# Tiled transformer-style block on one core: high and low tokens of a half go through one stationary tile as one matmul of two 256-column runs, in the output projection and the first FFN pairs

## The chip, the core and the metric

The kernel runs on one core of one Trainium2 chip. The engines that matter here are TensorE (PE in the rows; its weight loads are PEld), VectorE (DVE), ScalarE (ACT), GpSimd (POOL, which here issues transfers) and the queue of SyncE (SPq), which issues most transfers. The metric is the device time of one execution in microseconds, lower is better.

## What is computed

One layer over 512 latent tokens and 256 context tokens, 2048 channels wide, in fp32: modulation vectors from a conditioning vector, a token mixer (two parallel scans), an output projection, and a SwiGLU feed-forward network. What the change touches, cut from the reference:

```python
y = jnp.concatenate([y_m, y_r], axis=-1).astype(u.dtype) @ w_out          # output projection
x = x + m_lat[2] * rms_norm(yx, g_post_mix[layer])
hx = rms_norm(x, g_pre_ffn[layer]) * (1.0 + m_lat[4]) + m_lat[3]
gu = u @ w_ffn_in                                                          # u is hx
(jax.nn.silu(gu[..., :D_FF]) * gu[..., D_FF:]) @ w_ffn_out
```

`m_lat[2]` to `m_lat[5]` are products of the conditioning vector with four 2048-column blocks of `w_mod`.

## The kernel before

**Split products.** Every fp32 operand of a large product is kept as a high part and a low part in the type float32r, and a product is made of high times high, high times low and low times high. `aHL` holds the activations, [128, 2, 16, 512]: high (`aH`) and low (`aL`), 16 channel tiles, 512 tokens. A weight tile of 128 x 1024 comes into one of three buffers `wr` by a transfer on SyncE's queue; ScalarE casts it to `wH` (line 170), VectorE subtracts to get `wL` (line 186). There are four pairs `wH`/`wL`; the fourth is called `w3H`/`w3L`.

**Units.** One weight tile is one unit: eight stationary 128 x 128 blocks. In the stage of this change, tokens are worked in two halves of 256 (`halves`). The output projection has 32 units for each half (16 output tiles `o`, two units each, `j`), then the first FFN pairs have 24 units for each half (6 pairs `f`, gate and up, two units each): 112 units in all. `chunk` issues a unit of a half as 24 matmuls of 256 columns: for each of eight blocks the high weights with high tokens, then the same high weights with low tokens, and after these the low weights with high tokens. The results of tile `o` go to `wbank(o)`, which alternates between two PSUM banks (`bank_66` for even `o`, `bank_65` for odd `o`), so tile `o + 2` overwrites the bank of tile `o`. Later stages use `wide`, which issues a unit as 8 matmuls of 512 columns (high and low tokens of 256) and 8 of 256.

**Order.** Nothing is scheduled on the chip: the program is written out engine by engine while the kernel is built, and each engine runs its instructions in that order. What order results is decided by a small planner with a clock for each engine (`clk`). `spend` adds a fixed cost for each instruction. The main stream is the units; everything else is written as generators in lanes: `E` the evacuations of PSUM, `N` the norms and the modulation (`chain`, `sums`), `W` the modulation vectors (`mod_lane`). After about every 510 planner ns of matmul, `slot` asks each lane whether its next step is placed here:

```python
for n, lim in cur[0].rate:
    while lanes[n] and due(lanes[n][0]) and max(clk["dve"], clk["act"]) - clk["pe"] < lim:
        step(n)
```

In the output projection the limit of `W` is `RWO = 1053` and of `N` `RNO = 2600`. A step that is needed at once is forced with `until`, which places the whole lane up to a flag there. While unit `i` is written out, casts are placed up to unit `i + 3` and low parts up to unit `i + 2`.

**The `W` lane.** `mod_lane` streams `w_mod` through a single buffer `wm` of 512 KB. Each of its 128 half steps is one VectorE instruction (line 457), which multiplies `wm` in place and sums it, and then a transfer on SyncE's queue that fills `wm` again (line 462). The instruction waits for the transfer before it, and the transfer for the instruction before it. A step of the lane is two halves.

**The `N` lane in this stage.** `chain(0)` runs beside the projection of the second half: it normalizes the first half of the projection, adds the residual, writes it out to DRAM (`xdr`, line 1042), takes the sum of squares, makes the second norm, then calls

```python
yield from norm(pb, [nsum[:, 0:HALF], nsum[:, HALF:S]])
until("W", ("mod", 2))
```

and makes the new high and low tokens in eight steps, one for two channel tiles: one VectorE multiply, two activations and one cast on ScalarE, one VectorE subtract. The first FFN unit of a half is preceded by `until("N", ("u", hf))`. `chain(1)` runs beside the pairs of the first half in the same way.

Of the kernel before, what the change touches and what calls it, by code (L numbers as in the profile page):

```python
# [8 lines left out]
AF = mybir.ActivationFunctionType  # L9
ALU = mybir.AluOpType  # L10
# [4 lines left out]
S = 512  # L15
# [5 lines left out]
HALF = S // 2  # L21
# [55 lines left out]
def build(tc, A):  # L77
# [6 lines left out]
    with pool as sb, ppool as ps, dpool as dr, tc.manual_schedule():  # L84
        bank = [ps.tile([128, 512], F32, name=f"bank{i}") for i in range(8)]
        aHL = sb.tile([128, 2, KT, S], F32R, name="aHL")
        cHL = sb.tile([128, 2, 8, S], F32R, name="cHL")
        aH, aL = aHL[:, 0], aHL[:, 1]
# [25 lines left out]
        modv = sb.tile([128, 4, KT], F32, name="modv")  # L114
# [14 lines left out]
        yx = lambda o: ya[0][:, S * o:S * o + S] if o < 8 else sz[:, S * (o - 8):S * (o - 8) + S]  # L129
# [28 lines left out]
        def width(ap):  # L158
            n = 1
            for d in ap.shape[1:]:  # L160
                n *= d
            return n

        def act(out, in_, f, **kw):
            spend("act", 220 + 0.833 * width(in_) + (2560 if f in (AF.Sqrt, AF.Ln) else 0))
            SC.activation(out, in_, f, **kw)  # L166

        def acopy(out, in_):
            spend("act", 220 + 0.833 * width(in_))
            SC.copy(out, in_)  # L170
# [13 lines left out]
        def tt(out, a, b, op):  # L184
            spend("dve", 70 + 1.04 * width(out))
            V.tensor_tensor(out, a, b, op)  # L186
# [9 lines left out]
        def mm(out, l, r, st, sp):  # L196
            spend("pe", 0.424 * width(r) * (1 if r.dtype == F32R else 4))
            PE.matmul(out, lhsT=l, rhs=r, start=st, stop=sp)  # L198
# [143 lines left out]
        for q in range(4):  # L342
            t = (sa if q < 2 else sz)[:, 2048 * (q % 2):2048 * (q % 2) + 2048]
# [549 lines left out]
        def chunk(H, L, jobs, slot):  # L893
            Hv, Lv = (t.rearrange("p (k f) -> p k f", f=128) for t in (H, L))
            for part in range(2):
                for out, mov, ks, first, last in jobs:
                    n = len(ks)
                    for kk, k in enumerate(ks):
                        h, l = mov(k)
                        if part == 0:  # L900
                            mm(out, Hv[:, kk], h, first and kk == 0, False)
                            mm(out, Hv[:, kk], l, False, False)
                        else:
                            mm(out, Lv[:, kk], h, False, last and kk == n - 1)
                        if clk["pe"] >= mark[0] + GAP:
                            mark[0] = clk["pe"]
                            slot()

        def wide(H, L, out, mov, slot):
            Hv, Lv = (t.rearrange("p (k f) -> p k f", f=128) for t in (H, L))  # L910
            out2 = out.rearrange("p (t s) -> p t s", t=2)
            for part in range(2):
                for k in range(8):
                    if part == 0:
                        mm(out2, Hv[:, k], mov(k), k == 0, False)
                    else:
                        mm(out2[:, 0], Lv[:, k], mov(k)[:, 0], False, k == 7)
                    if clk["pe"] >= mark[0] + GAP:
                        mark[0] = clk["pe"]
                        slot()  # L920

        lat = lambda k: (uH(k), uL(k))
        latp = lambda hs: (lambda k: (aH[:, k, hs], aL[:, k, hs]))
        ctxm = lambda k: (cHv[:, k, :], cLv[:, k, :])

        def pre_last0():
# [40 lines left out]
        nacc, nsqe = eb[2:4], eb[12]  # L967
# [100 lines left out]
        wbank = lambda o: bank[(len(order) + o) % 2]  # L1068
        for hf, hs in enumerate(halves):
            for o in range(KT):  # L1070
                for j in range(2):
                    def emit(H, L, slot, o=o, hs=hs, j=j):
                        ks = range(8 * j, 8 * j + 8)
                        chunk(H, L, [(wbank(o)[:, 0:HALF], latp(hs), ks, j == 0, j == 1)], slot)

                    def pre(o=o, hf=hf, j=j):
                        if o == 0 and hf == 0 and j == 0:
                            until("W", ("mod", 0))
                            flush_e()
                            ysplit_y(range(8, 16), halves[0])  # L1080
                            lane("N", ysplit_rest())
                        if hf == 0 and j == 0 and o == 10:
                            until("N", ("y", 15))
                        if hf == 1 and j == 0 and o == 0:
                            until("N", ("y", 11))

                    def post(o=o, hf=hf, hs=hs, j=j):
                        if j == 0:
                            return

                        def g():
                            if o == 0 and hf == 0:
                                until("N", ("y", 13))
                            y, b = yx(o)[:, hs], wbank(o)[:, 0:HALF]
                            act(nacc[hf] if o == 0 else nsqe, b, AF.Square)
                            act(y, b, AF.Copy, scale=modv[:, 0, o:o + 1])
                            yield
                            if o:
                                tt(nacc[hf], nacc[hf], nsqe, ALU.add)
                            if o == KT - 1:  # L1100
                                lane("N", chain(hf, bank[7 - hf]))
                                if hf:
                                    lane("N", sums())
                        lane("E", g())
                    add(A["wout"][o, 1 - j], 1024, emit, pre, post, (("W", RWO), ("N", RNO)))


        def first_pair(f, hf, pb, pre0):
            hs = halves[hf]
            g = gtmp[:, HALF * (f % 2):HALF * (f % 2) + HALF]  # L1110
            h = stmp[:, HALF * (f % 2):HALF * (f % 2) + HALF]

            def swiglu():
                bg, bu = pb[0][:, 0:HALF], pb[1][:, 0:HALF]
                act(g, bg, AF.Silu)
                yield
                tt(h, g, bu, ALU.mult)
                PL.dma_start(out=hdr[:, f, hs], in_=h)

            for gu in range(2):  # L1120
                for j in range(2):
                    def emit(H, L, slot, gu=gu, j=j):
                        chunk(H, L, [(pb[gu][:, 0:HALF], latp(hs), range(8 * j, 8 * j + 8), j == 0, j == 1)], slot)

                    def post():
                        lane("E", swiglu())
                        if hf and f == FIRST - 1:
                            flags.add("halves")

                    add(A["ffin"][f, gu, j], 1024, emit, pre0 if not (gu or j) else None, post if gu and j else None, (("N", RNF),))  # L1130
# [261 lines left out]
        for g, fs in enumerate(groups):  # L1392
            last = g == len(groups) - 1
# [213 lines left out]
```

## Time and profile before

| | us |
|---|---|
| median of 3 runs (lowest to highest) | 2518.44 (2515.88 to 2526.44) |
| the profiled execution, its own time | 2522.63 |
| its span, first to last instruction | 2520.9 |
| PE busy in the span | 2458.5 |
| the stage of the change, 921.5 to 1260.44 | 338.94 |
| in that stage PE / DVE / ACT busy | 332.06 / 243.76 / 194.72 |

Between the profiled time and its span lie 1.7 us outside the first and last instruction. The stage is read from the first 256-column matmul on `aHL` of the output projection to the first 512-column matmul of the next stage. A matmul's recorded duration is longer than the distance to the next one, since matmuls are pipelined; the distance between starts is what a stream of them costs.

### The profile page before, as it was taken

What the parts mean: (1) busy time and instruction counts of PE and PEld (TensorE: products, weight loads), DVE (VectorE), ACT (ScalarE), POOL (GpSimd) and SP (SyncE); (2) the same over time, 40 slices, a digit from 0 to 9 for tenths busy, and PEclk for the clock granted to TensorE, in tenths of its full rate; (3) what the DMA queues carried; (4) which work ended last, traced back from release to release, by engine and by line L of the source; (5) the groups of instructions that cost most, each with busy time, mean ns of one, the idle gap of its engine ahead of it and who ended that gap; (6) DMA issues with size and microseconds to landing.
All of it is one profiled execution on the core that took longest, in us unless ns stands there. A gap on an engine that the chain in (4) does not pass through costs nothing. (4 is left out here: it accounts for less than half of the span.)

```text
span 2520.9 us, 36962 instructions
## 1 busy us (share of the span) xinstructions
PE 2458.5 (98%) x14504; PEld 2149.3 (85%) x14504; DVE 1776.1 (70%) x2830; ACT 1064.2 (42%) x1466; POOL 194.7 (8%) x300
## 2 busy tenths in 40 slices
PE   6999999999999999999999999999999999999997
PEld 4688888888888889999988888888888888888897
DVE  4477576676767866768688888888888866633357
ACT  4353344444445445566444343333443351221254
POOL 0010000000000020101011111111111120000000
PEclk9999999999999999999999999999999999999998
DMA  8954434434343477867676666666666586643345
GB/s 326 371 200 134 146 102 145 136 103 138 122 138 108 152 237 248 284 186 235 205 203 165 173 169 167 181 176 164 171 169 182 155 297 224 214 134 92 100 152 192
DMA packets 129743, 453.56 MB, mean 180 GB/s; under 512 B 15936, under 2 KB 20032, under 8 KB 128672
## 3 DMA queue, kind: packets, MB, share of 16 engines
q1 hardware_dynamic: 102128, 358.02, 43.2%
q0 software_dynamic: 27440, 93.17, 14.3%
q8 instruction: 114, 1.87, 0.3%
q14 instruction: 61, 0.50, 0.1%
HBM read 383.49 MB, written 27.79 MB: 163 GB/s over the span
## 5 line engine op out<-in xcount | busy, mean ns | idle before, releaser
L198 PE MATMUL bank<-aHL,wH 128*128 128x512 f32 (+1 forms) x4792 | 1007.0, 356 | 8.1 <-ACT sa L166 2.5
L198 PEld LDWEIGHTS bank<-aHL,wH 128*128 128x128 f32 x4792 | 782.2, 191 | 124.8 <-issue 6.1
L170 ACT CAST wH<-wr 128x1024 fp32r<-128x1024 f32 (+2 forms) x335 | 345.1, 1031 | 511.0 <-PE bank L198 305.7
L198 PE MATMUL bank<-aHL,wL 128*128 128x256 f32 (+1 forms) x2856 | 543.3, 326 | 0.6 <-DVE wL L186 0.6
L198 PEld LDWEIGHTS bank<-aHL,wL 128*128 128x128 f32 x2856 | 436.9, 191 | 49.8 <-DVE wL L186 1.0
L186 DVE TENSOR_TENSOR wL<-wr,wH 128x1024 fp32r<-128x1024 f32 (+2 forms) x335 | 400.3, 1197 | 41.6 <-ACT wH L170 38.9
L186 DVE TENSOR_TENSOR sz<-sz,bank 128x256 f32<-128x256 f32 (+1 forms) x678 | 301.3, 450 | 125.6 <-PE bank L198 100.6
L198 PE MATMUL bank<-cHL,wH 128*128 128x256 f32 (+1 forms) x1536 | 294.1, 338 | 7.5 <-DVE cHL L186 3.5
L198 PEld LDWEIGHTS bank<-cHL,wH 128*128 128x128 f32 x1536 | 240.1, 190 | 40.5 <-ACT wH L170 4.1
L170 ACT CAST wH<-sz 128x1024 fp32r<-128x1024 f32 (+1 forms) x126 | 129.7, 1047 | 245.8 <-DMA sz<-sz 170.0
L457 DVE CUSTOM_DVE_ANT_0 wm<-wm,sil 128x1024 f32<-128x1024 f32 x128 | 156.1, 1220 | 72.2 <-DMA wm<-wm 72.2
L186 DVE TENSOR_TENSOR sz<-sz 128x512 f32<-128x512 f32 (+2 forms) x220 | 155.7, 710 | 70.9 <-DMA sz<-sz 40.3
L198 PE MATMUL bank<-aHL,w3H 128*128 128x256 f32 (+1 forms) x1064 | 194.6, 333 | 0.0
L198 PEld LDWEIGHTS bank<-aHL,w3H 128*128 128x128 f32 x1064 | 161.1, 191 | 16.9
L198 PE MATMUL bank<-cHL,wL 128*128 128x256 f32 (+1 forms) x992 | 163.2, 302 | 0.0
L198 PEld LDWEIGHTS bank<-cHL,wL 128*128 128x128 f32 x992 | 144.1, 190 | 18.9 <-DVE wL L186 5.3
L186 DVE TENSOR_TENSOR wL<-sz,wH 128x1024 fp32r<-128x1024 f32 (+1 forms) x126 | 152.7, 1217 | 7.8 <-ACT wH L170 6.3
L170 ACT CAST w3H<-wr 128x1024 fp32r<-128x1024 f32 (+1 forms) x75 | 77.0, 1027 | 174.5 <-PE bank L198 83.4
L198 PE MATMUL bank<-aHL,w3L 128*128 128x256 f32 (+1 forms) x680 | 105.4, 298 | 0.0
L198 PEld LDWEIGHTS bank<-aHL,w3L 128*128 128x128 f32 x680 | 95.6, 191 | 6.6
L166 ACT ACT_TABLE_LOAD x61 | 78.3, 1283 | 35.5 <-PE bank L198 29.8
L186 DVE TENSOR_TENSOR w3L<-wr,w3H 128x1024 fp32r<-128x1024 f32 (+1 forms) x75 | 89.2, 1190 | 2.0 <-ACT w3H L170 2.0
(230 smaller groups left out, 2168.5 us busy)
## 6 DMA issues: line engine op xcount, KB each, us to landing
wm<-wm SPq DMA_DIRECT2D x134, 512.0 KB, 3.7
wr<-ffin SPq DMA_DIRECT2D x105, 512.0 KB, 4.5
wr<-ffout SPq DMA_DIRECT2D x96, 512.0 KB, 3.6
sz<-ffin SPq DMA_DIRECT2D x95, 512.0 KB, 4.8
wr<-win SPq DMA_DIRECT2D x85, 512.0 KB, 3.6
wr<-wout SPq DMA_DIRECT2D x64, 512.0 KB, 4.5
sz<-sz POOLq DMA_DIRECT2D x38, 512.0 KB, 5.2
wr<-wm SPq DMA_DIRECT2D x20, 512.0 KB, 8.9
```

Of the source, the lines that this page charges most:

```text
L166: SC.activation(out, in_, f, **kw)
L170: SC.copy(out, in_)
L186: V.tensor_tensor(out, a, b, op)
L198: PE.matmul(out, lhsT=l, rhs=r, start=st, stop=sp)
L457: V.tensor_tensor_reduce(out=wm, in0=wm, in1=sil[:, 1024 * j:1024 * j + 1024], scale=1.0, scalar=0.0, op0=ALU.mult, op1=ALU.add, accum_out ...
```

## The change

In the 112 units of the output projection and of the first FFN pairs, `chunk` is replaced by `wide`: high and low tokens of the half are one matmul of 512 columns (two runs of 256), so a unit has 8 matmuls of 512 columns and 8 of 256 in place of 24 of 256. `wide` gets two flags, so that a sum may go over two units. High-weight products with high tokens and with low tokens now lie in two halves of a PSUM bank and have to be added: the evacuation of a projection tile becomes a copy by ScalarE, an add by VectorE that reads the other half of the bank, and then the square and the scaled copy, both from SBUF; before, square and scaled copy read PSUM and VectorE had no part in it but the running sum. The evacuation of a pair gets two copies and two adds. Bytes moved and columns streamed stay as they are.

```diff
-        def wide(H, L, out, mov, slot):
+        def wide(H, L, out, mov, slot, first=True, last=True):
             Hv, Lv = (t.rearrange("p (k f) -> p k f", f=128) for t in (H, L))
             out2 = out.rearrange("p (t s) -> p t s", t=2)
             for part in range(2):
                 for k in range(8):
                     if part == 0:
-                        mm(out2, Hv[:, k], mov(k), k == 0, False)
+                        mm(out2, Hv[:, k], mov(k), first and k == 0, False)
                     else:
-                        mm(out2[:, 0], Lv[:, k], mov(k)[:, 0], False, k == 7)
+                        mm(out2[:, 0], Lv[:, k], mov(k)[:, 0], False, last and k == 7)
...
                     def emit(H, L, slot, o=o, hs=hs, j=j):
-                        ks = range(8 * j, 8 * j + 8)
-                        chunk(H, L, [(wbank(o)[:, 0:HALF], latp(hs), ks, j == 0, j == 1)], slot)
+                        wide(H, L, wbank(o), lambda k: aHL[:, :, 8 * j + k, hs], slot, j == 0, j == 1)
...
                             if o == 0 and hf == 0:
                                 until("N", ("y", 13))
-                            y, b = yx(o)[:, hs], wbank(o)[:, 0:HALF]
-                            act(nacc[hf] if o == 0 else nsqe, b, AF.Square)
-                            act(y, b, AF.Copy, scale=modv[:, 0, o:o + 1])
+                            y, b = yx(o)[:, hs], wbank(o)
+                            acopy(y, b[:, 0:HALF])
+                            yield
+                            tt(y, y, b[:, HALF:S], ALU.add)
+                            yield
+                            act(nacc[hf] if o == 0 else nsqe, y, AF.Square)
+                            act(y, y, AF.Copy, scale=modv[:, 0, o:o + 1])
                             yield
...
             def swiglu():
-                bg, bu = pb[0][:, 0:HALF], pb[1][:, 0:HALF]
-                act(g, bg, AF.Silu)
-                yield
-                tt(h, g, bu, ALU.mult)
+                for t, b in ((g, pb[0]), (h, pb[1])):
+                    acopy(t, b[:, 0:HALF])
+                yield
+                for t, b in ((g, pb[0]), (h, pb[1])):
+                    tt(t, t, b[:, HALF:S], ALU.add)
+                yield
+                act(g, g, AF.Silu)
+                yield
+                tt(h, g, h, ALU.mult)
                 PL.dma_start(out=hdr[:, f, hs], in_=h)
...
-                        chunk(H, L, [(pb[gu][:, 0:HALF], latp(hs), range(8 * j, 8 * j + 8), j == 0, j == 1)], slot)
+                        wide(H, L, pb[gu], lambda k: aHL[:, :, 8 * j + k, hs], slot, j == 0, j == 1)
```

Since the planner's clocks see other costs, the lanes' steps land elsewhere. Three places follow; units are counted from 0 at the first unit of the second half's projection, so the first pair begins with unit 32.

**SyncE's queue, projection of the second half.** `wr` are the weight buffers, `wm` the buffer of the `W` lane, `wout` and `ffin` the projection's and the pairs' weights. Before:

```order
L1429 DMA wr_77<-wout 128x1024
L1429 DMA wr_75<-wout 128x1024
L462 DMA wm<-wm 128x1024 x2
L1429 DMA wr_76<-wout 128x1024
L1429 DMA wr_77<-wout 128x1024
```

And with the change:

```order
L1436 DMA wr_77<-wout 128x1024
L1436 DMA wr_75<-wout 128x1024
L462 DMA wm<-wm 128x1024 x10
L1436 DMA wr_76<-ffin 128x1024
L1436 DMA wr_77<-ffin 128x1024
```

Ten refills of `wm` stand in a row where two did, and they have moved back from the middle of the half (12 loads of `wout` follow them before) to its end (none follows).

**VectorE at the same place**, from the low part of unit 16 before and of unit 28 with the change; `sz<-sa,bank_72` is the first modulation step of `chain(0)`, `sz<-sz,bank_66` the add that evacuates projection tile 12. Before:

```order
L186 TENSOR_TENSOR wL_82<-wr_75,wH_79 128x1024
L457 ISA wm,mp<-wm,sil 128x1024
L457 ISA mp 128x1
L457 ISA wm,mp<-wm,sil 128x1024
L457 ISA mp 128x1
L186 TENSOR_TENSOR modv<-mp 128x16
L186 TENSOR_TENSOR modv<-modv,bmod 128x16
L182 SCALAR_TENSOR_TENSOR modv<-modv,gains 128x16
L186 TENSOR_TENSOR sz<-sa,bank_72 128x512
L186 TENSOR_TENSOR sz<-sz 128x256
L186 TENSOR_TENSOR wL_83<-wr_76,wH_80 128x1024
```

With the change (the two rows of line 457 stand there ten times, with nothing between them):

```order
L186 TENSOR_TENSOR wL_82<-wr_75,wH_79 128x1024
L457 ISA wm,mp<-wm,sil 128x1024
L457 ISA mp 128x1
...
L186 TENSOR_TENSOR modv<-mp 128x16
L186 TENSOR_TENSOR modv<-modv,bmod 128x16
L182 SCALAR_TENSOR_TENSOR modv<-modv,gains 128x16
L186 TENSOR_TENSOR sz<-sa,bank_72 128x512
L186 TENSOR_TENSOR sz<-sz,bank_66 128x256
L186 TENSOR_TENSOR sz<-sz 128x256
L186 TENSOR_TENSOR wL_83<-wr_76,wH_80 128x1024
```

Eight more instructions of line 457 stand ahead of the add that frees `bank_66` and of the low part of unit 29. Of the 14 that the stage holds in either kernel, four are left that stand elsewhere in it.

**ScalarE, just before the pairs of the first half.** `sa<-sz,modv x2` and `CAST aHL` are one modulation step of `chain(0)`; `wH_81` and `w3H` are casts of weights. Before, they alternate:

```order
L170 CAST wH_81<-wr_77 128x1024
L166 ACTIVATE sz<-sz,modv 128x256 x2
L170 CAST aHL<-sz 128x2x256
L170 CAST w3H<-wr_75 128x1024
L166 ACTIVATE sz<-bank_65 128x256
L166 ACTIVATE sz<-bank_65,modv 128x256
L166 ACTIVATE sz<-sz,modv 128x256 x2
L170 CAST aHL<-sz 128x2x256
L170 CAST wH_79<-wr_76 128x1024
```

With the change all eight steps stand in one piece behind the casts of units 34 and 35 (six of them left out here):

```order
L170 CAST wH_81<-wr_75 128x1024
L170 CAST w3H<-wr_76 128x1024
L166 ACTIVATE sa<-sz,modv 128x256 x2
L170 CAST aHL<-sa 128x2x256
...
L166 ACTIVATE sz<-sz,modv 128x256 x2
L170 CAST aHL<-sz 128x2x256
L170 COPY sz<-bank_65 128x256
```

In `chain(1)`, at the pairs of the second half, the same has happened to five of eight steps: two stand behind the cast of unit 57, one behind that of unit 58, and five behind that of unit 59, where before each of the last five had a cast of weights behind it.

## Rows read from the trace of the kernel before

**Rows 1.** The page's first part: busy us of each engine.

```profile
PE 2458.5 (98%) x14504; PEld 2149.3 (85%) x14504; DVE 1776.1 (70%) x2830; ACT 1064.2 (42%) x1466; POOL 194.7 (8%) x300
```

**Rows 2.** Windows, the stage: us, busy PE, PEld, DVE, ACT, POOL, PEclk, DMA.

```profile
921.50:1260.44 338.94, 332.06 (x2730) 330.22 (x2729) 243.76 (x313) 194.72 (x287) 30.71 (x46) 0.99 0.71 232
```

**Rows 3.** Waits of PE, 900 to 1420: total us, times, longest.

```profile
PE bank L198 <- ACT sa L166: 2.5, 1, 2.5
```

**Rows 4.** Timeline of PE in the stage: start us, us, instruction.

```profile
1045.62 2.08 PE L198 MATMUL bank<-aHL,w3H 128*128 128x256 f32 x16
...
1057.14 2.08 PE L198 MATMUL bank<-aHL,w3H 128*128 128x256 f32 x16
```

**Rows 5.** Timeline of PE in the next stage, units issued by `wide`.

```profile
1402.92 2.00 PE L198 MATMUL bank<-ta,w3H 128*128 128x512 f32 x8
1404.76 1.12 PE L198 MATMUL bank<-ta,w3L 128*128 128x256 f32 x8
...
1425.26 2.00 PE L198 MATMUL bank<-cHL,w3H 128*128 128x512 f32 x8
```

**Rows 6.** Groups by line and shape: count, busy us, mean ns, idle before.

```profile
L186 DVE TENSOR_TENSOR sz<-sz,bank 128x256 f32<-128x256 f32 x598 | 247.0, 418 | 29.4 <-ACT sz L166 6.5 <-PE bank L198 6.4 <-DVE sz L186 0.5
...
L170 ACT COPY sz<-bank 128x256 f32<-128x256 f32 x62 | 22.9, 369 | 31.1 <-PE bank L202 21.2 <-PE bank L198 9.9
```

**Rows 7.** Timeline of all engines, 1056 to 1080: two `W` halves in a row.

```profile
1065.99 1.22 DVE L457 CUSTOM_DVE_ANT_0 wm<-wm,sil 128x1024 f32<-128x1024 f32 x1
...
1066.65 2.08 PE L198 MATMUL bank<-aHL,wH 128*128 128x256 f32 x16
1066.90 1.05 ACT L170 CAST wH<-wr 128x1024 fp32r<-128x1024 f32 x1 [2.17 <-PE bank L198]
...
1067.25 6.43 SPq L462 DMA_DIRECT2D wm<-wm  x2
...
1072.09 1.23 DVE L457 CUSTOM_DVE_ANT_0 wm<-wm,sil 128x1024 f32<-128x1024 f32 x1 [4.87 <-DMA wm<-wm]
...
1073.87 0.68 DVE L186 TENSOR_TENSOR sz<-sa,bank 128x512 f32<-128x512 f32 x1
1074.46 0.42 DVE L186 TENSOR_TENSOR sz<-sz 128x256 f32<-128x256 f32 x1
...
1074.80 2.35 DVE L186 TENSOR_TENSOR wL<-wr,wH 128x1024 fp32r<-128x1024 f32 x2
...
1077.64 1.12 PE L198 MATMUL bank<-aHL,wL 128*128 128x256 f32 x8
```

**Rows 8.** Timeline of DVE, 283 to 305: two `W` halves with nothing between.

```profile
290.03 1.22 DVE L457 CUSTOM_DVE_ANT_0 wm<-wm,sil 128x1024 f32<-128x1024 f32 x1 [4.28 <-DMA wm<-wm]
...
294.81 1.23 DVE L457 CUSTOM_DVE_ANT_0 wm<-wm,sil 128x1024 f32<-128x1024 f32 x1 [3.55 <-DMA wm<-wm]
```

**Rows 9.** Timelines of ACT and DVE, 1085 to 1120: one step of `chain(0)`.

```profile
1101.89 1.08 ACT L166 ACTIVATE sz<-sz,modv 128x256 f32<-128x256 f32 x2
1103.00 0.62 ACT L170 CAST aHL<-sz 128x512 fp32r<-128x512 f32 x1
1103.53 1.04 ACT L170 CAST wH<-wr 128x1024 fp32r<-128x1024 f32 x1
...
1106.36 0.68 DVE L186 TENSOR_TENSOR aHL<-sz,aHL 128x512 fp32r<-128x512 f32 x1
```

**Rows 10.** Timelines of PE at the first unit of each half's pairs.

```profile
1121.80 1.12 PE L198 MATMUL bank<-aHL,wH 128*128 128x256 f32 x8
...
1191.33 2.08 PE L198 MATMUL bank<-aHL,wH 128*128 128x256 f32 x16
```

**Rows 11.** Timeline of all engines, 1020 to 1047: the start of the second half.

```profile
1034.92 0.47 ACT L166 ACTIVATE sa<-bank,modv 128x256 f32<-128x256 f32 x1 [7.65 <-DMA xdr<-sa]
...
1035.44 3.62 PE L198 MATMUL bank<-aHL,wH 128*128 128x256 f32 x16 [2.55 <-ACT sa L166]
```

**Rows 12.** Windows at that place; the clock stands behind POOL's busy time.

```profile
1035.40:1037.00 1.60, 1.56 (x7) 1.56 (x8) 0.00 (x0) 1.58 (x3) 0.98 (x2) 0.50 0.99 374
```

More of the change, by code (lines that the diff above doesn't have):

```diff
@@ L922, in build @@
         lat = lambda k: (uH(k), uL(k))
-        latp = lambda hs: (lambda k: (aH[:, k, hs], aL[:, k, hs]))
         ctxm = lambda k: (cHv[:, k, :], cLv[:, k, :])
```

## Prediction

> **What bounds the kernel now.** I read the page's busy times first, then the windows of the stage that the change touches, then PE's waits in it, then its timeline. PE is busy for 98% of the span [rows 1] and for 332.1 of the stage's 338.9 us [rows 2]; the longest wait of PE in the stage is one of 2.5 us [rows 3]. So what the stage costs is the spacing of PE's matmuls, and everything else is paid only where PE is made to stand. VectorE (243.8 us) and ScalarE (194.7 us) have room on the average [rows 2]; the average says nothing of a place where one of them waits in its order.
>
> **What is removed: 896 matmuls.** Before, four units of 24 matmuls take 1057.14 - 1045.62 = 11.52 us, 2.88 us each, 120 ns a matmul [rows 4]. The next stage already issues units as `wide` does: eight of them take 1425.26 - 1402.92 = 22.34 us, 2.793 us each; a matmul of 512 columns costs (1404.76 - 1402.92)/8 = 230 ns where two of 256 cost 240 [rows 5]. The change puts 112 units from the one price to the other: 112 x 0.0875 = 9.8 us less. That is the whole direct gain, 0.39% of the time, since the columns stay.
>
> The Trainium skill has a rule that speaks for less (TensorE: Matmul & The Clock Gate, section Back-to-back issue gap): an isolated matmul of N columns takes N/2.4 ns and a fixed 2.5. By it a pair would save 2.5 ns and 896 of them 2.2 us, which would make the sum below 7.6 us longer. The trace disagrees: 230 against 240 ns.
>
> **What is added to the evacuations.** A copy of 256 columns from PSUM takes ScalarE 0.37 us, an add that reads PSUM takes VectorE 0.42 us [rows 6]. 32 projection tiles get one of each, 12 pairs two of each: 56 copies, 20.7 us, and 56 adds, 23.5 us, over the stage. ScalarE goes to 215 and VectorE to 267 of some 330 us, beside PE's matmuls, so I cost them at nothing; bare, the longer would be 23.5 us. But a bank is now freed by VectorE, where it was freed by ScalarE alone. Whatever holds VectorE up now holds PE up through the banks, two tiles later.
>
> **What is moved: eight halves of the W lane.** Here the order decides. With the change the planner finds no room for the `W` lane in most of the projection, and before the modulation of `chain(0)` it forces what is missing: ten halves on VectorE with nothing between, in place of two, and ten refills in a row on SyncE's queue. The buffer is single, so each half waits for a refill that waits for the half before it. What a reload costs stands in two rows. With two halves back to back the starts lie 294.81 - 290.03 = 4.78 us apart [rows 8]. At the place itself, where weight loads and other transfers run beside it, 1072.09 - 1065.99 = 6.10 us [rows 7]. In the new row, the loads of weights behind the ten refills can't be issued, so the queues run empty after the first; I take 4.78 and keep 6.10 for the range. Nine reloads are 43.0 us. From the start of the last half to the first modulation step are 1073.87 - 1072.09 = 1.78 us, that step takes 0.59 to the next start, the add 0.42 [rows 7]: tile 12's bank is free 45.8 us after the first half began.
>
> The Trainium skill (DMA: Bandwidth & Descriptors, section Anatomy of one DMA) gives about 2.0 us and the bytes at 436 GB/s for one transfer, 3.2 us for 512 KB, on GpSimd's path. With that in place of the wait of 3.55 us the sum would be 3.2 us shorter; no run here shows it for this queue.
>
> What can PE do in that time? Before, the row of halves began 0.66 us before the first matmul of the unit it is written in (1066.65 - 1065.99), which was unit 14 [rows 7]. Now it stands behind the low part of unit 28, so it is written in unit 26. With the same lead PE has 0.66 us and units 26 and 27, 2 x 2.79: 6.25 us. Then unit 28, the first of tile 14, overwrites `bank_66`, and the add that empties it stands behind the ten halves. PE stands 45.8 - 6.25 = **39.6 us**; with 6.10 us a reload 51.5. Queued behind the halves are also the low parts of units 29 and up, and ScalarE, whose square of tile 12 waits for the add and has the casts of units 30 and 31 behind it. The row of two cost nothing before, because only a low part hung on it: that of unit 17 was made from 1074.80, about 1.2 us long, and used at 1077.64, 1.6 us to spare; its cast had been there since 1068 [rows 7], so the low part did wait for VectorE's turn.
>
> **What is late next.** `chain(0)` now modulates in one piece, right before the pairs that read it. A step costs ScalarE 1103.53 - 1101.89 = 1.64 us, a subtract on VectorE 0.69 behind it [rows 9]. The eight steps stand behind the cast of unit 35 (1.05 us), which needs unit 31's buffer: they begin 1.05 us after PE has done all it had. The last tokens are there after 1.05 + 8 x 1.64 + 0.69 = 14.9 us; two 512-column matmuls and eight low ones follow, 0.46 + 0.96, and units 32 and 33 are done at 16.3 us where 5.6 would do: **10.7 us**. Were the steps 2.8 us earlier it would be 7.9; were all eight awaited, 14.9. Before, PE went into both halves' pairs without a wait [rows 10].
>
> At the second half's pairs the broadcast of the norm ends 3.8 us before unit 55 does; its first step on ScalarE begins 1.0 us later, and eight steps and the casts of units 58 and 59 (0.95 us each) take 15.0: 12.2 us after unit 55, plus 0.69 and 1.4: 14.3 against 5.6, **8.7 us** (5.8 to 12.9 by the same two bounds).
>
> At the start of the second half PE already stands for 2.55 us, behind a ScalarE instruction that waited 7.65 us for the write-out of the residual [rows 11]. With the change the bank is free after copy and add (0.79 us) in place of the scaled copy (0.47), and the norm's broadcast stands behind nine matmuls of unit 2, 1.96 us later in PE's order: **2.3 us** more, at least nothing.
>
> **Clock.** After that wait of PE the granted clock is 0.50, that is 1.2 GHz [rows 12], and 16 matmuls take 3.62 us [rows 11] where they take 2.08 [rows 4]: 1.5 us. Three new stands: **4.5 us** (3 if one is short, 9 if it costs double after a long one).
>
> **Sum.** -9.8 + 39.6 + 10.7 + 8.7 + 2.3 + 4.5 = +56.0 us. The profiled execution took 2522.6 us (span 2520.9 and 1.7 around it) and would take 2578.6. It lies 4.2 us above the median of the runs, so against the median I forecast 2518.4 + 56.0 = **2574 us**, its own range 2562 to 2596 by the bounds above.
>
> **Rivals.**
> - *The row of halves costs, the chains hide.* If ScalarE runs ahead during PE's long stand and both chains come in time, the last three waits and two of the clock terms go: -9.8 + 39.6 + 1.5, 2550 us. For it: no wait there before [rows 10]. Against it: the casts ahead of the steps need buffers that PE frees last.
> - *The reload stays at 6.10 us.* 11.9 us more, 2586. For it, the row at the place itself [rows 7]; against it, its other transfers are stuck behind.
> - *The 512-column form saves nothing here.* Weights and tokens are those of `aHL` as in the next stage, so I hardly believe it: 2584.
> - *Faster.* The halves are covered and only the spacing changes: 2518.4 - 9.8 = 2509. It is decided by the number of reloads: PE's stand is 4.78 n + 2.8 - 6.25, which eats the 9.8 us at the third. It would take VectorE to be some 40 us ahead of PE when the row begins. Two halves in a row were hidden before with 1.6 us to spare [rows 7]; nine reloads stand there now.
>
> **How the numbers follow.** The forecast 0.74, the chains hidden 0.10, the slow reload 0.09, no saving 0.03, faster 0.04. The range reaches from the chains hidden to the slow reload with its bounds: 2548 to 2596. A change below 0.5% (12.6 us) could hardly be told from none; the 9.8 us alone would lie there, as would part of the fourth case, so faster 0.03, same 0.03, slower 0.94.
>
> **What would show it.** The stage's units at 2.79 us, 16 matmuls each. On VectorE ten rows of line 457, some 4.8 us apart, with idle time put down to the refill; one wait of PE near 40 us on VectorE, `bank_66`, after which the clock is 0.50. PE waits of some 1 us each on `aHL` in the first two units of either half's pairs. Wrong would be: no long wait of PE although the ten rows stand there, a bank freed before the add, or reloads well under 4 us.

## The result, and the profile after

| | before | with the change |
|---|---|---|
| median, us (lowest to highest) | 2518.74 (2515.88 to 2526.44) | 2605.89 (2599.49 to 2610.43) |
| the profiled execution, its span | 2522.63, 2520.9 | 2610.43, 2608.7 |

The ratio is 1.0326, 95% interval 1.0306 to 1.0347: 87 us slower, where 56 were forecast. The time lies outside the stated range of 2548 to 2596.

The page's first part, of the changed kernel, answers to [rows 1]: PE's share falls from 98% to 95%, with 896 matmuls fewer.

```profile
PE 2477.9 (95%) x13608; PEld 2111.0 (81%) x13608; DVE 1799.6 (69%) x2886; ACT 1087.8 (42%) x1522; POOL 195.2 (7%) x300
```

Its windows (columns as in [rows 2]): the stage, from its first unit to the first unit of the next stage; two short windows behind waits; and the longest wait.

```profile
923.50:1324.92 401.42, 340.48 (x1833) 292.46 (x1833) 262.22 (x364) 217.20 (x340) 29.99 (x45) 0.90 0.59 195
...
1092.00:1094.00 2.00, 2.00 (x9) 1.71 (x8) 1.38 (x2) 1.34 (x3) 0.00 (x0) 0.50 0.25 80
...
1111.60:1151.20 39.60, 0.21 (x2) 0.01 (x1) 11.61 (x23) 0.00 (x0) 0.00 (x0) 0.54 0.34 108
1151.40:1153.00 1.60, 1.60 (x4) 1.31 (x5) 1.26 (x2) 1.57 (x3) 0.00 (x0) 0.50 0.60 243
```

The stage took 338.94 us [rows 2] and takes 401.4. VectorE and ScalarE did get about the busy time forecast for them (262 and 217 us, against 267 and 215).

PE's waits in the changed kernel (total us, times, longest): first in the stage, then, below the dots, in the next stage, 1325 to 2072.

```profile
PE bank L198 <- DVE sz L186: 44.1, 3, 39.5
PE bank L198 <- DVE aHL L186: 13.9, 13, 2.6
PE bank L198 <- DVE sa L186: 2.7, 1, 2.7
...
PE bank L198 <- ACT wH L170: 9.8, 19, 0.9
PE bank L198 <- ACT w3H L170: 3.8, 5, 1.3
```

The reader is to see the one wait of 39.5 us that was forecast; the thirteen on `aHL`, eleven of them at the first pairs as forecast and two at the stage's start, where PE had such waits before, too; and two dozen short ones behind the stage that were not forecast. In that next stage before:

```profile
PE bank L198 <- ACT wH L170: 2.4, 4, 1.0
PE bank L198 <- ACT w3H L170: 0.7, 2, 0.5
```

The timeline of all engines in the changed kernel, at two places in order of time: unit 22 of the second half's projection, then the row of ten halves.

```profile
1082.44 2.00 PE L198 MATMUL bank<-aHL,wH 128*128 128x512 f32 x8
...
1085.24 2.00 PE L198 MATMUL bank<-aHL,wH 128*128 128x512 f32 x8
1085.57 1.05 ACT L170 CAST wH<-wr 128x1024 fp32r<-128x1024 f32 x1 [3.55 <-DMA wr<-wout]
...
1086.65 1.23 DVE L186 TENSOR_TENSOR wL<-wr,wH 128x1024 fp32r<-128x1024 f32 x1 [3.58 <-ACT wH L170]
...
1087.60 0.36 ACT L170 COPY sz<-bank 128x256 f32<-128x256 f32 x1
1087.80 0.68 DVE L186 TENSOR_TENSOR sz<-sz 128x512 f32<-128x512 f32 x1
1088.51 0.63 ACT L166 ACTIVATE sz<-sz 128x512 f32<-128x512 f32 x1 [0.55 <-DVE sz L186]
1089.17 0.69 DVE L186 TENSOR_TENSOR sz<-sz 128x512 f32<-128x512 f32 x1 [0.69 <-ACT sz L166]
1089.78 0.41 DVE L186 TENSOR_TENSOR sz<-sz,bank 128x256 f32<-128x256 f32 x1
...
1090.34 2.97 PE L198 MATMUL bank<-aHL,wH 128*128 128x512 f32 x7 [2.15 <-DVE sz L186]
...
1104.31 1.22 DVE L457 CUSTOM_DVE_ANT_0 wm<-wm,sil 128x1024 f32<-128x1024 f32 x1
...
1105.56 44.49 SPq L462 DMA_DIRECT2D wm<-wm  x10
...
1110.71 1.23 DVE L457 CUSTOM_DVE_ANT_0 wm<-wm,sil 128x1024 f32<-128x1024 f32 x1 [5.18 <-DMA wm<-wm]
...
1115.58 1.23 DVE L457 CUSTOM_DVE_ANT_0 wm<-wm,sil 128x1024 f32<-128x1024 f32 x1 [3.63 <-DMA wm<-wm]
...
1148.47 1.23 DVE L457 CUSTOM_DVE_ANT_0 wm<-wm,sil 128x1024 f32<-128x1024 f32 x1 [3.48 <-DMA wm<-wm]
...
1150.84 0.42 DVE L186 TENSOR_TENSOR sz<-sz,bank 128x256 f32<-128x256 f32 x1
...
1151.31 3.78 PE L198 MATMUL bank<-aHL,wH 128*128 128x512 f32 x8 [39.50 <-DVE sz L186]
```

Undisturbed units are 2.80 us apart (1085.24 - 1082.44). The halves run from 1104.31 to 1148.47 with their refills between, the add at 1150.84 frees `bank_66`, and PE goes on. At unit 22 the same happens on a small scale: the copy is done at 1087.96, but the add that frees the bank stands behind two steps of `chain(0)` on VectorE, one of which waits for ScalarE. These began late themselves: VectorE had just waited 3.58 us for a cast, and the cast 3.55 us for a weight tile.

PE's timeline in the changed kernel: the first unit of the first half's pairs, one matmul pair of the second half's first unit, and two units of the next stage seven apart.

```profile
1167.25 0.73 PE L198 MATMUL bank<-aHL,wH 128*128 128x512 f32 x2 [2.56 <-DVE aHL L186]
1168.89 0.93 PE L198 MATMUL bank<-aHL,wH 128*128 128x512 f32 x2 [0.92 <-DVE aHL L186]
1170.54 1.22 PE L198 MATMUL bank<-aHL,wH 128*128 128x512 f32 x2 [0.72 <-DVE aHL L186]
...
1253.22 1.22 PE L198 MATMUL bank<-aHL,wH 128*128 128x512 f32 x2 [1.35 <-DVE aHL L186]
...
1357.78 2.12 PE L198 MATMUL bank<-cHL,wH 128*128 128x512 f32 x8 [0.71 <-ACT wH L170]
...
1378.52 2.12 PE L198 MATMUL bank<-cHL,wH 128*128 128x512 f32 x8 [0.67 <-ACT wH L170]
```

PE's units come in the same order in both kernels, so the first matmul of each unit in one trace can be set against that in the other. What each stretch costs more than before, beyond the 0.0875 us saved in each of its units, is this:

| stretch | forecast | measured |
|---|---|---|
| spacing of 112 units | -9.8 | -9.8 |
| first half's projection (at its start) | 0 | +1.6 |
| start of the second half | +2.3 | +0.3 |
| units 13 and 14, which the norm's small matmuls have left | 0 | -1.3 |
| units 22 and 23, with the clock at 0.50 | 0 | +6.4 |
| row of ten halves, with the clock behind it | +39.6 +1.5 | +42.2 |
| first pairs of the first half | +10.7 +1.5 | +11.3 |
| other pairs of that half | 0 | -2.0 |
| norm ahead of the second half's pairs | 0 | +4.4 |
| first pairs of the second half | +8.7 +1.5 | +9.4 |
| the stage | +56.0 | +62.5 |
| the next stage, in which nothing was changed | 0 | +24.0 |

With 2.0 us by which the two executions differ ahead of the stage and -0.7 behind the next one, that is the difference of the spans, 87.8 us. Of the 24.0 us, 4.9 are lost in the next stage's first ten units and 19.1 behind them. The single stretches are those of one execution: in e13 below, which holds the same stage, units 22 and 23 cost 2.0 us in place of 6.4, the row with its clock 45.2 in place of 42.2, and the stage takes 397.0 us.

### The profile page after: what moved, and what is told of

It reads as the page before. It is cut to its first block, busy times and chain, and to the rows that moved or that the text cites. A ratio compares the mean times of both kernels' runs of the same rounds, so it can differ in the third digit from the quotient of the medians.

```text
span 2608.7 us, 35290 instructions
## 1 busy us (share of the span) xinstructions
PE 2477.9 (95%) x13608; PEld 2111.0 (81%) x13608; DVE 1799.6 (69%) x2886; ACT 1087.8 (42%) x1522; POOL 195.2 (7%) x300
## 5 line engine op out<-in xcount | busy, mean ns | idle before, releaser
L198 PEld LDWEIGHTS bank<-aHL,wH 128*128 128x128 f32 x4120 | 739.0, 191 | 207.0 <-DVE sz L186 39.7
L198 PEld LDWEIGHTS bank<-aHL,wL 128*128 128x128 f32 x2856 | 446.3, 192 | 57.1 <-DVE wL L186 0.8
L186 DVE TENSOR_TENSOR sz<-sz,bank 128x256 f32<-128x256 f32 (+1 forms) x706 | 312.3, 449 | 131.8 <-PE bank L198 94.7
L186 DVE TENSOR_TENSOR sz<-sz 128x512 f32<-128x512 f32 (+2 forms) x232 | 161.4, 696 | 84.4 <-DMA sz<-sz 52.7
L198 PE MATMUL bank<-aHL,w3H 128*128 128x512 f32 (+1 forms) x840 | 192.6, 375 | 0.0
L198 PEld LDWEIGHTS bank<-aHL,w3H 128*128 128x128 f32 x840 | 145.9, 190 | 24.2
L166 ACT ACTIVATE sz<-sz 128x512 f32<-128x512 f32 (+3 forms) x128 | 69.4, 544 | 121.8 <-DVE sz L186 86.7
```

## The experiments

Four questions: is it the order or the new work; the projection or the pairs; the row or the chains; and what slows the next stage. For the last one the **step** is read: the time of seven units, over 246 units from the eleventh of the next stage on. It is (1985.67 - 1288.39)/246 x 7 = 19.84 us before, 20.39 with the change; an unhindered step is 7 x 2.793 = 19.55.

**e1: new work, old order.** The copies and adds are issued without telling the planner; the pairs' evacuation likewise.

```diff
-                            acopy(y, b[:, 0:HALF])
-                            yield
-                            tt(y, y, b[:, HALF:S], ALU.add)
-                            yield
+                            SC.copy(y, b[:, 0:HALF])
+                            V.tensor_tensor(y, y, b[:, HALF:S], ALU.add)
```

> The changed kernel's instructions, but the planner is not told of the new copies and adds, so all engines keep the order of before: the row of ten halves is two again, and the steps of the N chains alternate with casts. Theory A (the order costs the time): no wait of 39.5 us on bank_66 and none of the waits at the first pairs; the form saves 9.8 us: 2509 to 2515 us. Theory B (the copies and adds themselves hold PE up, in whatever order): over 2545 us. Theory C (the 24 us that the changed kernel loses behind the stage come from the last pairs' longer evacuation, which holds back a low part and a weight load): waits of 1 us in every seventh unit of the next stage stay, and the time is 2525 to 2533 us.

Measured 2564.94 us, ratio 1.0157 (1.0135 to 1.0178). Waits of PE in and around its stage, then one place in its timeline:

```profile
PE bank L198 <- DVE sa L1094: 5.7, 6, 2.6
PE bank L198 <- DVE sz L186: 5.6, 3, 2.0
PE bank L198 <- issue: 4.6, 1, 4.6
PE bank L198 <- DVE aHL L186: 4.0, 4, 2.2
PE bank L198 <- DVE sz L1094: 3.7, 3, 2.2
```

```profile
1065.64 1.05 ACT L170 CAST wH<-wr 128x1024 fp32r<-128x1024 f32 x1 [1.97 <-DMA wr<-wout]
...
1066.60 0.36 ACT L1093 COPY sa<-bank 128x256 f32<-128x256 f32 x1
...
1066.99 0.42 DVE L1094 TENSOR_TENSOR sa<-sa,bank 128x256 f32<-128x256 f32 x1 [1.33 <-ACT sa L1093]
...
1067.47 2.11 PE L198 MATMUL bank<-aHL,wH 128*128 128x512 f32 x8 [1.01 <-DVE sa L1094]
```

No wait of 39.5 us, yet 43 us slower: theory A falls as the whole of it, and theory B holds in part. Here the copy stands behind a cast that waits for a weight tile, the add (line 1094) behind the copy, and PE behind the add. PE waits for such an add nine times, 9.4 us in all; at four of them a cast that waited for its tile stands right before the copy. The stage takes 360.8 us, 21.9 more than before; what makes up the rest was not taken apart. The next stage loses 25.6. That one might come from the last pairs' evacuation (C) is taken up by e2 and e3.

**e2: old work, new order.** The kernel before, with the planner charged for a copy and an add in each evacuation (two of each for a pair):

```diff
                             y, b = yx(o)[:, hs], wbank(o)[:, 0:HALF]
+                            spend("act", 220 + 0.833 * HALF)
+                            yield
+                            spend("dve", 70 + 1.04 * HALF)
+                            yield
```

> The instructions of before (24 matmuls of 256 columns, ScalarE evacuates), but the planner is charged with the copies and adds of the change, so the order is that of the changed kernel, with the row of ten halves. Theory A: slow without any of the new work: PE stands about 35 us, 4.8 less than in the changed kernel, since here ScalarE frees the banks and PE gets to the low part of unit 29 before it needs VectorE; 9.8 us are not saved: 2600 to 2616 us. Theory B: about 2519 us. Theory C: the stage behind loses little, so 24 us less than by theory A: 2577 to 2592 us.

Measured 2578.06 us, ratio 1.0216 (1.0194 to 1.0238). Waits of PE in its stage, and below the dots the largest in its next stage:

```profile
PE bank L198 <- DVE wL L186: 35.7, 1, 35.7
PE bank L198 <- ACT aHL L170: 6.6, 8, 3.5
PE bank L198 <- DVE aHL L186: 4.7, 9, 1.0
...
PE bank L198 <- ACT wH L170: 1.0, 3, 0.5
```

The row of ten stops the old kernel for 35.7 us, at the low part and not at the bank, as expected. The stage takes 398.7 us, 59.8 more than before, from the order alone. The next stage takes 724.4 us, 725.2 before: nothing is lost there, so neither the long wait nor the chains cause that loss. That is why the time lies in theory C's range, which supposed it, and below theory A's.

**e3 and e4: one part alone.** In e3 the projection gets its old lines back, in e4 the pairs (one of the places of e3):

```diff
-                        wide(H, L, wbank(o), lambda k: aHL[:, :, 8 * j + k, hs], slot, j == 0, j == 1)
+                        ks = range(8 * j, 8 * j + 8)
+                        chunk(H, L, [(wbank(o)[:, 0:HALF], latp(hs), ks, j == 0, j == 1)], slot)
```

> The change in the first pairs alone; the projection as before. The row of halves stays at two. Theory A: saves 48 x 0.0875 = 4.2 us, and only the steps of the second chain, half of which now stand without casts between, can cost some us: 2514 to 2524 us. Theory C: the loss behind the stage is here in full: 2535 to 2545 us.

> The change in the output projection alone; the pairs as before. The row of ten halves is here. Theory A: stand of 39.5 us and the forced first chain stay, 4.2 us of saving are lost, the second chain costs less; the stage behind loses its 24 us as well if it is the stands that cause it: 2595 to 2610 us. Theory C: the stage behind loses nothing: 2570 to 2585 us.

e3: 2523.57 us, ratio 1.0007 (0.9997 to 1.0018); the 4.2 us are given back at the second half's norm and first pairs. Its next stage loses 3.3 us, so theory C falls as the account of the whole loss: the pairs' new evacuation is here in full and the loss is not. A part of it stands. In the next stage's first ten units the seven kernels with the new evacuation in the pairs lose 2.9 to 6.2 us (e3 3.6, the changed kernel 4.9), those with the old one 0 to 1.8 (e7 0.2), save e11 with 6.0. e4: 2582.39 us, ratio 1.0239 (1.0219 to 1.0260), below theory A's range, with a wait of 41.3 us at the bank; its next stage loses 7.9. The row comes with the projection alone; the loss behind the stage comes in full with neither part.

**e5: the row taken apart.** One number in the changed kernel:

```diff
-RWO = 1053
+RWO = 3000
```

> The changed kernel with one number changed: the limit of the W lane in the projection is 3000 in place of 1053, which spreads the halves (14 single refills on SyncE's queue, no row). The modulation of both chains still stands in one piece. Theory A (the row of ten is the 39.5 us): the wait on bank_66 goes, with the 2 us of low clock behind it; the waits at the first pairs (10 and 9 us) and the loss behind the stage (24 us) stay: 2560 to 2570 us. If the loss behind the stage hung on the long stand, 2537 to 2545 us. If VectorE's total work were the limit, the stand would only be spread: over 2590 us.

Measured 2566.51 us, ratio 1.0175 (1.0156 to 1.0195), inside theory A's range. The stage falls from 401.4 to 361.7 us. Waits of PE in it:

```profile
PE bank L198 <- DVE aHL L186: 17.4, 17, 3.3
PE bank L198 <- DVE sz L186: 12.6, 2, 12.2
```

The sum is as expected, its parts are not quite: a wait of 12.2 us for the norm of `chain(0)` now stands just ahead of the first pairs. During the long wait that chain had been given its time for nothing. Of the 24 us behind the stage that were expected to stay, 17.4 did.

**e7: the form alone.** 512-column matmuls, evacuations as before, reading only the half with the high tokens (in the pairs likewise).

```diff
-                            acopy(y, b[:, 0:HALF])
-                            yield
-                            tt(y, y, b[:, HALF:S], ALU.add)
-                            yield
-                            act(nacc[hf] if o == 0 else nsqe, y, AF.Square)
-                            act(y, y, AF.Copy, scale=modv[:, 0, o:o + 1])
+                            act(nacc[hf] if o == 0 else nsqe, b[:, 0:HALF], AF.Square)
+                            act(y, b[:, 0:HALF], AF.Copy, scale=modv[:, 0, o:o + 1])
```

> The 512-column form alone: the evacuations are those of before and read only the half of the bank with the products of the high tokens, so the products of high weights and low tokens are computed and left out of the result. No copies, no adds, order and other engines' instructions as before. The form saves 9.8 us in the stage: 2509 to 2513 us. By theory D the next stage is slow here too, with none of the new work: 20.4 us a step, 2530 to 2537 us.

Measured 2540.87 us, ratio 1.0073 (1.0058 to 1.0088). The stage takes 332.3 us, 6.6 less than before: the 9.8 are there, 3.2 go in small waits, 2.2 of them at the norm ahead of the second half's pairs. (The same stage in e9, e10, e14 and e15 is 2.8 to 5.5 us shorter than before.) But the next stage takes 753.4 us, 28 more, at 20.64 us a step, though ScalarE, VectorE and both transfer queues run the same instructions there in the same order as before. PE's waits in it:

```profile
PE bank L198 <- ACT wH L170: 16.1, 20, 1.9
PE bank L198 <- ACT w3H L170: 3.9, 4, 1.4
```

So neither the order nor the new evacuation is needed for the loss behind the stage. Without a copy, an add or a new order, the form alone makes the kernel 17 us slower.

**e8: ScalarE frees the bank.** The projection alone, planner not told, pairs as before:

```diff
-                            acopy(y, b[:, 0:HALF])
-                            yield
-                            tt(y, y, b[:, HALF:S], ALU.add)
+                            q = nacc[hf] if o == 0 else nsqe
+                            SC.copy(y, b[:, 0:HALF])
+                            SC.copy(q, b[:, HALF:S])
+                            yield
+                            V.tensor_tensor(y, y, q, ALU.add)
```

> The change in the projection alone, with the planner not told, and ScalarE copies both halves of the bank, so that it frees the bank as before and VectorE adds in SBUF. Theory B' (what the new evacuation costs in the order of before is that PE waits for banks behind VectorE): these waits go, 5.6 us are saved by the form: 2513 to 2521 us. If it is the added work on ScalarE and VectorE by itself: over 2535 us.

Measured 2557.41 us, ratio 1.0130 (1.0113 to 1.0147). Theory B' falls: PE now waits ten times, 7.3 us, for ScalarE's second copy. Its stage takes 358.4 us, 19.5 more than before, and its next stage loses 19.5. So it is not which engine frees the bank; before seven of the ten waits the copies stand behind a cast that waited for its weight tile. That the added work on ScalarE and VectorE costs by itself, the other branch (over 2535 us), fits; where in the order it does was not taken apart.

**e6, e9, e10, e11: the next stage and TensorE's program.** e6 is e1 with matmuls of one column ahead of everything, e10 is e7 with half as many there; e9 is e7 with them behind everything. e11 is the kernel before without the products of high weights and low tokens in the stage.

```diff
+        for _ in range(896):
+            PE.matmul(bank[7][:, 0:1], lhsT=ident, rhs=one, start=True, stop=True)
```

> The kernel that keeps the order of before, with 896 matmuls of one column put in at its start, so that TensorE's program is as long as before the change; its time is longer by these and says nothing. What is read is the step of the next stage, seven units: 19.84 us before, 20.40 us in the changed kernel and in the one with the order of before. Theory D (what slows the transfers there hangs on the length or place of TensorE's program, which falls from 14504 matmuls to 13608): 19.8 us. If it hangs on how the stage before ends: 20.4 us.

> The 512-column form alone (products of high weights and low tokens left out of the result) with 896 matmuls of one column behind all other work, so that TensorE's program is as long as before, and every instruction up to the end of the next stage stands where it stands in the form alone. What is read is the step of seven units in the next stage: 20.64 us in the form alone, 19.84 before. Theory D1 (it hangs on the place of an instruction in TensorE's program): 20.6 us. Theory D2 (it hangs on the length of the whole program): 19.8 us.

> The 512-column form alone (the same products left out of the result) with 448 matmuls of one column at the start, half of what was put in to restore the length. Theory D in any form: between 19.8 and 20.6 us a step if it goes with the length, either of the two if it goes with an alignment. If the start of the program or its delay is what helped, and not the length: 19.8 us.

> The kernel before, without the 896 matmuls of high weights and low tokens in the output projection and the first pairs (left out of the result); no matmul of 512 columns there, no copy, no add, order as before. TensorE's program has 13608 matmuls, as with the change. Theory D: the next stage takes 20.4 to 20.6 us a step though nothing of the change is in it. If the 512-column form or the new evacuation is the cause: 19.8 us.

The step: e6 19.80, e9 19.97, e10 19.83, e11 20.16 us. A matmul of one column in fp32 is two in the trace, so that e6 and e9 have 15400 matmuls, more than before, and it is e10 that has 14504. e10's next stage takes 725.2 us, that of before. D1 falls with e9, where no instruction up to there has moved. e11 has nothing of the change in it, and its next stage loses 17.3 us, 6.0 of them in its first ten units; its step is above that of before, but under the 20.4 that theory D named. So in these runs the loss goes with how long TensorE's program is, and neither the program's start nor the form is needed to account for it.

**e12: the pairs alone, planner not told.** As e3, with the edit of e1 in the pairs (the copies shown, the adds likewise).

```diff
-                    acopy(t, b[:, 0:HALF])
-                yield
+                    SC.copy(t, b[:, 0:HALF])
```

> The change in the first pairs alone, with the planner not told of the copies and adds, so that the second chain's steps alternate with casts as before. Saves 48 x 0.0875 = 4.2 us, and the waits of some 7 us that stood at the second half's pairs and its norm when the planner was told should go: 2516 to 2520 us, against 2522 before.

Measured 2531.08 us, ratio 1.0044 (1.0028 to 1.0060): wrong. Each against its runs of the kernel before, it is 10.5 us slower and e3 1.2: the planner's own order for the new work is better than the old order with the work put in unseen. In the profiled execution 2.9 us are lost in the stage and 6.2 in the next stage's first ten units; the step, 19.86 us, is that of before.

**e13, e14, e15: what of the program.** The changed kernel with the 896 matmuls of e9 behind everything; e7 with 1792 copies of one column on ScalarE behind everything (`SC.copy(small[:, 0:1], cst[:, 2:3])`); e7 with one more DRAM tensor.

> The changed kernel, complete, with 896 matmuls of one column behind all other work, so that TensorE's program is as long as before. Its time is longer by these and says nothing; what is read is the step of seven units in the next stage (20.39 us in the changed kernel, 19.84 before) and the time from the stage's first unit to the end of the next stage. Theory D2 (the length of the program): 19.8 to 20.0 us a step, and some 15 to 20 us less up to the end of the next stage; stage itself as in the changed kernel, with the wait of 39.5 us. Otherwise 20.4 us.

> The 512-column form alone (products of high weights and low tokens left out of the result), with 1792 copies of one column on ScalarE behind all other work: as many instructions as 896 matmuls with their weight loads, but in another engine's program. If the length of all programs together, or where memory is laid out behind them, sets the step of the next stage: 19.8 to 20.0 us. If it is TensorE's own program: 20.6 us, as in the form alone.

> The 512-column form alone (the same products left out of the result) with one more DRAM tensor of 128 KB, of which a few bytes are written at the end. If the layout of the kernel's own DRAM tensors sets the step of the next stage, it moves from 20.6 us towards 19.8; if not, 20.6 us.

The step: e13 20.01, e14 20.29, e15 20.42 us. In e13 the changed kernel's next stage falls from 749.3 to 734.0 us, though the long wait is there (41.9 us). A longer ScalarE program (e14) or one more tensor (e15) takes 0.35 and 0.22 us off e7's step, where half the matmuls took 0.81 (e10) and e9's took 0.67. e14 lies at neither of the two values expected. What helps most is TensorE's program; each figure is from one execution.

No kernel here is faster than the one before.

## Why the prediction was wrong, and where it was right

**The spacing: right.** Units are 2.80 us apart in the changed kernel, and e7's stage is 6.6 us shorter. By the rule for an isolated matmul in the Trainium skill (TensorE: Matmul & The Clock Gate, section Back-to-back issue gap) only 2.2 us were to be had, an estimate, with units at 2.86 us; the trace disagrees again.

**The row of halves: right in place and mechanism, in size partly by luck.** Ten halves, 4.7 us apart after the first, one wait of 39.5 us on `bank_66` against 39.6 forecast. The two agree so closely because two misses cancel: the nine reloads took 44.2 us where 43.0 were reckoned, and PE had 7.5 us of work where 6.25 were. In e13 the same wait is 41.9 us. e2 has the wait without the change's work, e5 the change's work without the wait. The slow reload of 6.10 us came once, for the first refill (6.40 us from start to start), while weight loads still ran. The waits for the other refills are 3.4 to 3.6 us. By the Trainium skill (DMA: Bandwidth & Descriptors, section Anatomy of one DMA) 3.2 us come out for one of this size on another path, an estimate; the trace's waits are 0.2 to 0.4 above it.

**The forced chains: right.** 11.3 and 9.4 us with the clock, against 12.2 and 10.2. That they hide behind the long wait did not happen, but e5 shows that the wait did hide another 12.2 us of `chain(0)`.

**Start of the second half: mis-sized.** 2.3 us forecast, 0.3 measured.

**"I cost them at nothing": wrong.** The prediction put the copies and adds beside PE's matmuls because ScalarE and VectorE have room on the average. It named the coupling itself (whatever holds VectorE up holds PE up through the banks) and then priced it at one place only. At unit 22 PE waits 2.15 us for an add, and with the clock at 0.50 behind the wait units 22 and 23 cost 6.4; 0.9 of that are the norm's small matmuls, which cost as much at unit 13 before. In e13, where the weight tile ahead of it came 1.3 us earlier in PE's order, the same wait is 0.85 us, the clock stays at 1.00, and the two units cost 2.0: what such a place costs hangs on the transfers, too. The 4.4 at the second half's norm and the 1.6 at the stage's start are no waits for a bank: there PE waits 2.45 us for the norm's sum (0.84 at its old place), and for `aHL`. In the new order the new work costs 401.4 - (398.7 - 6.6) = 9.3 us, in the old one 360.8 - 332.3 = 28.5 (e1 against e7), from single executions of stages that differ by some 4 us between executions: the planner's new order also saves something.

**The failing step: the sum ended with the stage.** It was made of the stage's own terms, with all behind it taken as unchanged, since the rows there stand as before. 24.0 us were lost there, more than the forecast's whole error in the stage (6.5); without them the time would lie inside the stated range. 4.9 of them stand in the next stage's first ten units, where the kernels with the pairs' new evacuation lose time (e3); the prediction had that evacuation at nothing, too. 19.1 come in its steps, at transfers that land later, and their cause stays open. No row of the profile before gave these; they could only have been held open as a range.

The forecast's own rivals are all out: both chains came late, reloads after the first took 4.7 us, the units are 2.80 us apart, and PE stood through the row.

## What to carry to other kernels

When an evacuation gets a second engine, price the wait at each place where that engine's queue holds something that itself waits; the share of busy time says nothing on it. Where a planner sets the order, read the new order for rows of the same single-buffered step: nine reloads were worth four times the whole gain, and their price could be read from two rows (4.78 us where eight of them took 4.72, and 6.10 where the first took 6.40). And compare the traces behind the change as well as in it: a stage that nobody touched lost over a quarter of the difference.

## What the runs showed of the hardware that was not expected

The next stage's step sorts by the number of TensorE's matmuls in the program: 19.77 to 20.01 us in eight kernels with 14120 or more (mean 19.86), 20.16 to 20.64 in seven with 13608 (mean 20.36), 20.02 and 20.39 in the two with 13992. Over the stage's 35 steps the means differ by 17 us. What gets slower is the transfers. In the changed kernel PE's wait of 0.71 us at 1357.78, shown above, follows a cast that waited for one:

```profile
1356.68 1.05 ACT L170 CAST wH<-sz 128x1024 fp32r<-128x1024 f32 x1 [10.64 <-DMA sz<-sz]
```

Issues in the next stage (tile, queue, count, KB each, median us to landing), in the changed kernel:

```profile
wr<-ffin SPq DMA_DIRECT2D x54, 512.0 KB, 7.3
sz<-sz POOLq DMA_DIRECT2D x36, 512.0 KB, 6.7
```

and in e10, where the length is restored:

```profile
wr<-ffin SPq DMA_DIRECT2D x54, 512.0 KB, 6.0
sz<-sz POOLq DMA_DIRECT2D x36, 512.0 KB, 5.7
```

The same transfers at the same places in the order take about 1 us longer (6.4 and 5.8 before). Each ends in sixteen landings, and worked out from the trace's landing events the last comes, on the mean, 0.8 us behind the eighth before, 0.9 in e10, 1.2 with the change and 1.5 in e7: a part of the sixteen comes late. This follows the step only roughly: in e13 the last is 1.2 us behind with a step of 20.01, and in e11 1.4 us with 20.16 and medians of 6.5 and 5.8. Whether it is the length of TensorE's program that does this, and how, was not settled. The steps above are from one profiled execution for each kernel; the timed runs of e7 stayed within 6 us, but those of the kernel before spread over 17 (2512.01 to 2529.39 us, beside e9 to e12). That a program between 13608 and 14120 matmuls can be on either side (e4, e8) says that length may stand for something else that goes with it, such as where the program lies in memory, which no run here tested.
